# A mixture-of-experts block: the experts' token rows through DRAM tables by indirect DMA in place of one-hot matrices

## The chip, the cores and the metric

One core of one Trainium2 chip runs the whole program; the other cores are idle. The metric is the device time of one execution in microseconds. Three runs of the kernel before took 1461.52, 1463.50 and 1463.19 us; the median is 1463.19.

## The reference

Two transformer layers over 256 tokens of width 1024, in float32: a stick-breaking attention with a dense SwiGLU, then a softmax attention with a mixture of eight experts, then a norm. Only the mixture matters here:

```python
def moe_swiglu(h, w_router, w1, w3, w2):
    t = h.reshape(b * s, d)                       # 256 x 1024
    logits = jnp.dot(t, w_router)                 # 256 x 8
    top_val, top_idx = lax.top_k(logits, TOP_K)   # 2 of 8 experts
    top_w = jax.nn.softmax(top_val, axis=-1)
    gates = jnp.einsum('tk,tke->te', top_w, jax.nn.one_hot(top_idx, N_EXPERTS))

    def expert(args):
        e_w1, e_w3, e_w2, g = args                # 1024x3584, 1024x3584, 3584x1024
        hid = jax.nn.silu(t @ e_w1) * (t @ e_w3)
        return (hid @ e_w2) * g[:, None]
    y = jnp.sum(lax.map(expert, (w1, w3, w2, gates.T)), axis=0)
```

The reference runs all tokens through all experts; a token counts only in its two.

## The kernel before

**Splits.** Each float32 weight tile of 128x1024 is split into a high part (`wh`, ScalarE, line 153) and the remainder (`wl`, VectorE, line 154), and each product is three matmuls of 128x512 (`mm3`, lines 175 to 177): high by high, high by low, low by high. `wh` and `wl` have four buffers each, so the splits run at most four tiles ahead of TensorE.

**Weights.** `jobs` lists the weight loads in the order of use, mostly 1 MB each. `stream()` takes them, and `load_ahead()` issues on SP (line 129) as many as there are buffers `raw`: 9 at first, one more before the second attention (`RING1`), 3 (`RING3`) within it, and 4 (`RING2`) at its end, 17 during the experts. A load waits until VectorE has split the former tile in its buffer. 337 loads belong to the experts, 42 to each whole one.

**Experts.** The core keeps the tokens in two blocks `b` of 128, `hn[b]`, and 128 slots for the tokens of each expert. `slot[:, b, e]` is a token's number within expert `e`, counted from 1, or 0. For expert `e`, `gather()` compares it to `iota` (`mark`, line 808), which gives the one-hot matrix `pe`, and multiplies the blocks by it (line 815), so that the expert's rows come out transposed in PSUM; `split_out` brings them into `eh` and `el`. Each of an expert's seven chunks `i` of 512 hidden columns then does 48 matmuls for `e_w1` and `e_w3`, and 24 for `e_w2` of the chunk before (`down`), into the banks `y`; `hid_t` transposes the hidden tile (line 594). The last chunk of an expert also runs `gather()` of the next. `slots()` transposes `pe` into `pt` (line 845) and works out the gate of each slot (line 847). The first chunk of the next expert ends with `scatter()`: `split_y` multiplies `y` by the gates and splits it (lines 857, 858), eight matmuls by `pt` (lines 870, 871) bring the rows back to their tokens, and four additions (line 872) put them into `ht`. The last expert's rows are scattered after the loop.

**Overflow.** Where an expert has more than 128 tokens, `rest()` runs afterwards under a branch on `most_v` (line 991). With these inputs it doesn't run.

**Order.** The program's text gives the order of dependences; a planner with a simulated timeline places the instructions on each engine's queue, and may move them ahead of ones written earlier. `behind()` fixes an order by hand. GpSimd's queue carries the small loads, the bias tiles and the `rv_d` table.

Of the kernel before, what the change touches and what calls it, by code (L numbers as in the profile page):

```python
# [10 lines left out]
F32 = mybir.dt.float32  # L11
F32R = mybir.dt.float32r
BF16 = mybir.dt.bfloat16
AF = mybir.ActivationFunctionType
ALU = mybir.AluOpType
PSUM = bass.MemoryType.PSUM

P = 128
D = 1024
S = 256  # L20
NB = S // P
# [4 lines left out]
NE = 8  # L26
DFE = 3584
FC = 512
# [2 lines left out]
N_BUCKETS = 32  # L31
MAX_DISTANCE = 128
RING = 9
RING1, RING2, RING3 = 1, 4, 3
GRAN = 2048
HALF = GRAN // 2
NV = 384
WARM = 6
WARMS = 1, 1, 1
MIDDLE = 6  # L40
PUMPS = (7, 7), (7, 7), (7, 7), (7, 7), (2, 3), (2, 3), (1, 3), (2, 2), (2, 2)


@with_exitstack
def block_kernel(ctx: ExitStack, tc: tile.TileContext, x, w_qkv, w_o, mixer_norm, ffn_norm,
                 rel_bias, w1, w3, w2, router, e_w1, e_w3, e_w2, final_norm, onehot, out):
    nc = tc.nc
# [9 lines left out]
    bank = [psp.tile([P, FC], F32, name=f"bank{i}") for i in range(8)]  # L57
# [122 lines left out]
    def split_out(src, h, l):  # L180
        return (nc.scalar.activation(h, src, AF.Copy),  # L181
                nc.vector.tensor_sub(l, src, h.bitcast(F32)))
# [55 lines left out]


    rv_d = dramp.tile([NH, P, NV], F32, name="rv_d")  # L240

    rb = op0.tile([N_BUCKETS, NH], F32, name="rb", bufs=1)
    nc.gpsimd.dma_start(rb, rel_bias)
# [416 lines left out]
    hold = hold[2:]  # L660
    nc.gpsimd.dma_start(rv_d, rv.unsqueeze(1).to_broadcast([NH, P, NV]))
    layer0.close()
    with tc.tile_pool(name="fp", bufs=4) as fp:
        dense_ffn(fp, hold, lambda b: hold.append(norm_t(b, 1)))

# [136 lines left out]
                                           gate[:, b], op0=ALU.mult, op1=ALU.add)  # L802


    def gather(e, banks, later):

        def mark(b):
            return nc.vector.tensor_scalar(pe[:, b], iota, slot[:, b, e:e + 1], None,
                                           op0=ALU.is_equal)

        def part(b, i, later):
            ps = bank[banks[i]]
            for c in range(4):
                cc = 4 * i + c
                i0 = nc.tensor.matmul(ps[:, c * P:(c + 1) * P], hn[b][:, cc * P:(cc + 1) * P],
                                      pe[:, b].bitcast(F32), start=b == 0 and c == 0,
                                      stop=b == NB - 1 and c == 3, skip_group_check=True)
                behind((i0, later))

        def done(i):  # L820
            split_out(bank[banks[i]], eh[:, 4 * i:4 * i + 4].rearrange("p c t -> p (c t)"),
                      el[:, 4 * i:4 * i + 4].rearrange("p c t -> p (c t)"))

        mark(0)
        if e == 0:
            part(0, 0, later)
            later = numbers(1)
            part(0, 1, later)
            held[1] = mark(1)
            for i in range(2):  # L830
                part(1, i, later)
                done(i)
        else:
            mark(1)
            for i in range(2):
                for b in range(NB):
                    part(b, i, later)
                done(i)

    def slots(e):  # L840

# [31 lines left out]
        return i0, i1  # L873

    pend, done = None, None
    gather(0, (3, 4), raws[2])
    k = 0
    most_v = None
    pos2 = mp.tile([P, NB, NE], F32, name="pos2")

    for e in range(NE):
        for i, (f0, n) in enumerate(ecs):
            b1, b3 = (5, 6) if k % 2 == 0 else (3, 4)
            k += 1
            for bk in (b1, b3):
                if bk == b3:
                    held[:] = None, None
                for c, w in enumerate(stream(NC, hold=held)):
                    _, last = mm3(bank[bk], (eh[:, c], el[:, c]), w, c == 0, c == NC - 1)
                if pend is not None and bk == b1:  # L890
                    hT = hid_t(pend[1], FC, bank[pend[2]], *hts)
            if i == len(ecs) - 1 and e + 1 < NE:
                gather(e + 1, (2, 7), last)
            t = gate_mul(ep.tile([P, FC], F32, name="nat"), bank[b1], bank[b3], n)
            if pend is not None:
                for j, w in enumerate(stream(4)):
                    down(y, hT, j, w, pend[0] == 0, pend[0] == len(ecs) - 1)
            pend = (i, t, b1)
            if i == 0:
                if done is not None:  # L900
                    scatter(done)
                else:
                    gates()

                    cps = bank[2]
                    for b in range(NB):
                        nc.tensor.matmul(cps[:, :NE], ones, sel[:, b], start=b == 0,
                                         stop=b == NB - 1)
                    most = mp.tile([P, 1], F32, name="most")
                    nc.vector.tensor_reduce(most, cps[:, :NE], axis=mybir.AxisListType.X,  # L910
                                            op=ALU.max)
                    most_i = mp.tile([P, 1], mybir.dt.int32, name="most_i")
                    nc.vector.tensor_copy(most_i, most)
                    nc.vector.tensor_scalar(pos2, slot, -float(P), None, op0=ALU.add)
                done = slots(e)
    hT = hid_t(pend[1], FC, bank[pend[2]], *(sp[0][:, i * FC:(i + 1) * FC] for i in range(2)))

    row = ep.tile([P, FC], F32, name="nat")
# [143 lines left out]
```

## Time and profile before

| | |
|---|---|
| median of three runs | 1463.19 us |
| profiled execution | 1468.19 us, of which the span from first to last instruction is 1466.5 |
| attention 0, dense layer, attention 1 and routing | 0 to about 460 us |
| eight experts | about 460 to 1447 us |
| last scatter, norm and store | to 1466.5 us |
| TensorE, VectorE, ScalarE busy in 600 to 1340 us | 740.0, 679.4, 578.6 us |
| bytes by DMA | 430 MB, 293 GB/s over the span |

One execution is profiled, so its own time stands beside its span. Busy TensorE is not TensorE at its peak: matmuls overlap, and a 128x512 one is shown with 0.39 us where the next starts 0.23 us later. What an instruction costs TensorE is read from the start of one to the start of the next.

### The profile page before, as it was taken

What the parts mean: (1) busy time and instruction counts of PE and PEld (TensorE: products, weight loads), DVE (VectorE), ACT (ScalarE), POOL (GpSimd) and SP (SyncE); (2) the same over time, 40 slices, a digit from 0 to 9 for tenths busy, and PEclk for the clock granted to TensorE, in tenths of its full rate; (3) what the DMA queues carried; (4) which work ended last, traced back from release to release, by engine and by line L of the source; (5) the groups of instructions that cost most, each with busy time, mean ns of one, the idle gap of its engine ahead of it and who ended that gap; (6) DMA issues with size and microseconds to landing.
All of it is one profiled execution on the core that took longest, in us unless ns stands there. A gap on an engine that the chain in (4) does not pass through costs nothing. (4 is left out here: it accounts for less than half of the span.)

```text
span 1466.5 us, 20171 instructions
## 1 busy us (share of the span) xinstructions
PE 1447.3 (99%) x7553; PEld 1221.5 (83%) x7553; DVE 1203.5 (82%) x1421; ACT 1036.6 (71%) x1303; POOL 21.1 (1%) x44
## 2 busy tenths in 40 slices
PE   9999999999999999999999999999999999999996
PEld 7877999988878888888888888888888888888885
DVE  6555766667667998999999899899999989989995
ACT  6556655546565887787777778777877877877784
POOL 1000000000000000000000000000000000000000
PEclk9999999999998999999999999999999999999998
DMA  9962555556567999999999999999999999999920
GB/s 326 215 235 87 194 186 195 186 178 231 168 229 248 373 366 356 346 368 365 340 345 380 350 348 363 353 344 362 371 348 342 372 355 344 377 360 329 365 92 31
DMA packets 168619, 429.80 MB, mean 293 GB/s; under 512 B 6866, under 2 KB 8946, under 8 KB 154436
## 3 DMA queue, kind: packets, MB, share of 16 engines
q1 hardware_dynamic: 166852, 422.61, 79.9%
q0 software_dynamic: 1600, 5.84, 2.5%
q8 instruction: 61, 1.00, 0.3%
q14 instruction: 42, 0.34, 0.1%
q10 hardware_dynamic: 64, 0.02, 0.0%
HBM read 424.24 MB, written 4.19 MB: 292 GB/s over the span
## 5 line engine op out<-in xcount | busy, mean ns | idle before, releaser
L154 DVE TENSOR_TENSOR wl<-raw,wh 128x1024 fp32r<-128x1024 f32 x710 | 850.6, 1223 | 110.6 <-ACT wh L153 89.3
L153 ACT ACTIVATE wh<-raw 128x1024 fp32r<-128x1024 f32 x710 | 746.3, 1061 | 206.6 <-PE bank L177 165.1
L176 PE MATMUL bank<-wl,oh_t 128*128 128x512 f32 x968 | 377.7, 391 | 0.0
L175 PE MATMUL bank<-wh,oh_t 128*128 128x512 f32 x968 | 374.8, 396 | 0.5 <-ACT oh_t L181 0.5
L177 PE MATMUL bank<-wh,oh_t 128*128 128x512 f32 x904 | 353.6, 391 | 4.0 <-PEq L991 4.0
L176 PEld LDWEIGHTS bank<-wl,oh_t 128*128 128x128 f32 x968 | 182.3, 188 | 38.8 <-DVE wl L154 0.2
L175 PEld LDWEIGHTS bank<-wh,oh_t 128*128 128x128 f32 x968 | 182.9, 189 | 37.9 <-ACT oh_t L181 1.1
L177 PEld LDWEIGHTS bank<-wh,oh_t 128*128 128x128 f32 x904 | 170.4, 189 | 40.3 <-issue 4.2
L177 PE MATMUL bank<-wh,ol_t 128*128 128x512 f32 x504 | 194.4, 391 | 0.0
L162 DVE SCALAR_TENSOR_TENSOR wl<-raw,gcol,wh 128x512 fp32r<-128x512 f32 (+1 forms) x192 | 131.1, 726 | 72.7 <-ACT wh L161 72.3
L161 ACT ACTIVATE wh<-raw,gcol 128x512 fp32r<-128x512 f32 (+1 forms) x192 | 123.9, 699 | 93.6 <-PE bank L313 54.3
L176 PE MATMUL bank<-wl,ol_t 128*128 128x512 f32 x440 | 173.0, 393 | 0.0
L313 PE MATMUL bank<-x_h,wh 128*128 128x256 f32 x512 | 144.7, 283 | 3.4 <-ACT t L435 3.4
L313 PE MATMUL bank<-x_h,wl 128*128 128x256 f32 x512 | 143.8, 281 | 0.0
L313 PE MATMUL bank<-x_l,wh 128*128 128x256 f32 x512 | 143.4, 281 | 0.0
L175 PE MATMUL bank<-wh,ol_t 128*128 128x512 f32 x440 | 140.9, 391 | 0.0
L177 PEld LDWEIGHTS bank<-wh,ol_t 128*128 128x128 f32 x504 | 94.4, 188 | 20.4 <-issue 1.1
L313 PEld LDWEIGHTS bank<-x_h,wh 128*128 128x128 f32 x512 | 96.7, 189 | 5.5 <-ACT t L435 3.6
L313 PEld LDWEIGHTS bank<-x_h,wl 128*128 128x128 f32 x512 | 96.9, 189 | 0.0
L175 PEld LDWEIGHTS bank<-wh,ol_t 128*128 128x128 f32 x440 | 82.6, 188 | 17.1
L313 PEld LDWEIGHTS bank<-x_l,wh 128*128 128x128 f32 x512 | 96.7, 189 | 0.2
L176 PEld LDWEIGHTS bank<-wl,ol_t 128*128 128x128 f32 x440 | 82.9, 188 | 14.9
(199 smaller groups left out, 1201.5 us busy)
## 6 DMA issues: line engine op xcount, KB each, us to landing
raw<-in_e_w_dram SPq DMA_DIRECT2D x335, 1024.0 KB, 6.9
raw<-in_w_dram SPq DMA_DIRECT2D x33, 1024.0 KB, 5.0
raw<-in_w_qkv_dram SPq DMA_DIRECT2D x22, 1024.0 KB, 5.6
raw<-in_w_o_dram SPq DMA_DIRECT2D x8, 1024.0 KB, 9.5
rv_d<-rv POOLq DMA_DIRECT2D x1, 3072.0 KB, 36.2
raw<-in_w_qkv_dram SPq DMA_DIRECT2D x4, 512.0 KB, 7.6
bias<-rv_d POOLq DMA_DIRECT2D x8, 256.0 KB, 4.3
h<-in_x_dram SPq DMA_DIRECT2D x4, 256.0 KB, 6.2
```

Source lines behind the costliest of these rows:

```text
L153: i0 = nc.scalar.activation(wh[:, :m], src, AF.Copy)
L154: i1 = nc.vector.tensor_sub(wl[:, :m], src, wh[:, :m].bitcast(F32))
L161: i0 = nc.scalar.activation(wh[:, cs], src[:, cs], AF.Copy, scale=gc)
L162: i1 = nc.vector.scalar_tensor_tensor(wl[:, cs], src[:, cs], gc, wh[:, cs].bitcast(F32), op0=ALU.mult, op1=ALU.subtract)
L175: i0 = nc.tensor.matmul(ps, s[0], m[0], start=start, stop=False)
L176: nc.tensor.matmul(ps, s[0], m[1], start=False, stop=False)
L177: i1 = nc.tensor.matmul(ps, s[1], m[0], start=False, stop=stop)
L313: nc.tensor.matmul(to, w[a][:, ms], z[:, :, c], start=c + i + m % 2 == 0, stop=c == NC - 1 and m % 2 == 1 and i == 2, skip_group_check=True)
```

## The change

Rows of tokens go through two tables in DRAM. `xs_d` has 128 rows for each of the eight experts, `ys_d` for the first seven. After the first attention `xs_d` is cleared from `hn[1]`, which is free then. Once the slots are known (chunk 0 of expert 0), `send()` works out for each token and each of its two experts the row `128 e + slot - 1` (out of bounds where the slot is above 128) and writes the rows of `hn` there by four indirect DMAs. Expert 1 and later ones load their 128 rows in a plain DMA (`load_x`, in chunk 1 of the expert before), and `turn_x()` transposes them on TensorE, 8 transposes, where `gather()` stood. `store_y()` copies an expert's result to SBUF and stores it in `ys_d`, for experts 0 to 6. In expert 7, `fetch()` clears two tiles and gathers each token's rows by its two row numbers (rows of expert 7 are out of bounds and stay zero), and `add_rows()` adds them, times the gates, to `ht`: block 0 asked for in chunk 2 and added in chunk 3, block 1 in 3 and 4. Expert 0 still gathers, and expert 7 still marks, makes slots and scatters by one-hot matrices. One weight buffer is given up for the two row tiles (`RING2` 4 to 3).

```diff
--- before.py
+++ after.py
@@ -31,13 +31,14 @@
 N_BUCKETS = 32
 MAX_DISTANCE = 128
 RING = 9
-RING1, RING2, RING3 = 1, 4, 3
+RING1, RING2, RING3 = 1, 3, 3
 GRAN = 2048
 HALF = GRAN // 2
 NV = 384
 WARM = 6
 WARMS = 1, 1, 1
 MIDDLE = 6
+FAR = 4096
 PUMPS = (7, 7), (7, 7), (7, 7), (7, 7), (2, 3), (2, 3), (1, 3), (2, 2), (2, 2)
 
 
@@ -238,6 +239,9 @@
 
 
     rv_d = dramp.tile([NH, P, NV], F32, name="rv_d")
+
+    xs_d = dramp.tile([NE * P, D], F32, name="xs_d")
+    ys_d = dramp.tile([(NE - 1) * P, D], F32, name="ys_d")
 
     rb = op0.tile([N_BUCKETS, NH], F32, name="rb", bufs=1)
     nc.gpsimd.dma_start(rb, rel_bias)
@@ -660,6 +664,10 @@
     hold = hold[2:]
     nc.gpsimd.dma_start(rv_d, rv.unsqueeze(1).to_broadcast([NH, P, NV]))
     layer0.close()
+
+    nc.gpsimd.memset(hn[1], 0.0)
+    nc.gpsimd.dma_start(xs_d.rearrange("(e p) d -> p e d", p=P),
+                        hn[1].unsqueeze(1).to_broadcast([P, NE, D]))
     with tc.tile_pool(name="fp", bufs=4) as fp:
         dense_ffn(fp, hold, lambda b: hold.append(norm_t(b, 1)))
 
@@ -802,11 +810,69 @@
                                            gate[:, b], op0=ALU.mult, op1=ALU.add)
 
 
-    def gather(e, banks, later):
-
-        def mark(b):
-            return nc.vector.tensor_scalar(pe[:, b], iota, slot[:, b, e:e + 1], None,
-                                           op0=ALU.is_equal)
+    place = mp.tile([P, NB, NE], F32, name="pos2")
+    row_in = mp.tile([P, 2, NB], mybir.dt.uint32, name="row_in")
+
+    def send():
+
+        nc.gpsimd.iota(rank, pattern=[[0, NB], [P, NE]], base=-1, channel_multiplier=0,
+                       allow_small_or_imprecise_dtypes=True)
+        nc.vector.tensor_scalar(place, slot, float(P), float(FAR), op0=ALU.is_gt, op1=ALU.mult)
+        nc.vector.tensor_add(place, place, slot)
+        nc.vector.tensor_add(place, place, rank)
+        nc.vector.tensor_mul(top, isk, place.unsqueeze(1).to_broadcast([P, 2, NB, NE]))
+        nc.vector.tensor_reduce(tv, top, axis=mybir.AxisListType.X, op=ALU.add)
+        nc.vector.tensor_copy(row_in, tv)
+        for b in range(NB):
+            for k in range(2):
+                nc.gpsimd.indirect_dma_start(
+                    xs_d, bass.IndirectOffsetOnAxis(ap=row_in[:, k, b:b + 1], axis=0), hn[b],
+                    None, bounds_check=NE * P - 1, oob_is_err=False)
+
+    def fetch(b, k):
+
+        t = ep.tile([P, D], F32, name="xr" if k == 0 else "yr")
+        nc.gpsimd.memset(t, 0.0)
+        nc.gpsimd.indirect_dma_start(
+            t, None, ys_d, bass.IndirectOffsetOnAxis(ap=row_in[:, k, b:b + 1], axis=0),
+            bounds_check=(NE - 1) * P - 1, oob_is_err=False)
+        return t
+
+    def add_rows(b, ts):
+        for k, t in enumerate(ts):
+            nc.vector.scalar_tensor_tensor(ht[b], t, ex[:, 1 + k, b:b + 1], ht[b], op0=ALU.mult,
+                                           op1=ALU.add)
+
+    def load_x(e):
+        t = ep.tile([P, D], F32, name="xr")
+        nc.gpsimd.dma_start(t, xs_d[e * P:(e + 1) * P])
+        return t
+
+    def store_y(e):
+        t = ep.tile([P, D], F32, name="yr")
+        nc.scalar.activation(t[:, :FC], y[0], AF.Copy)
+        nc.vector.tensor_copy(t[:, FC:], y[1])
+        nc.gpsimd.dma_start(ys_d[e * P:(e + 1) * P], t)
+
+
+    def mark(e, b):
+        return nc.vector.tensor_scalar(pe[:, b], iota, slot[:, b, e:e + 1], None, op0=ALU.is_equal)
+
+    def take(i, bk):
+        split_out(bank[bk], eh[:, 4 * i:4 * i + 4].rearrange("p c t -> p (c t)"),
+                  el[:, 4 * i:4 * i + 4].rearrange("p c t -> p (c t)"))
+
+    def turn_x(t, banks, later):
+
+        for i in range(2):
+            for c in range(4):
+                cc = 4 * i + c
+                behind((nc.tensor.transpose(bank[banks[i]][:, c * P:(c + 1) * P],
+                                            t[:, cc * P:(cc + 1) * P], ident), later))
+            take(i, banks[i])
+
+    def gather(banks, later):
+
 
         def part(b, i, later):
             ps = bank[banks[i]]
@@ -817,25 +883,14 @@
                                       stop=b == NB - 1 and c == 3, skip_group_check=True)
                 behind((i0, later))
 
-        def done(i):
-            split_out(bank[banks[i]], eh[:, 4 * i:4 * i + 4].rearrange("p c t -> p (c t)"),
-                      el[:, 4 * i:4 * i + 4].rearrange("p c t -> p (c t)"))
-
-        mark(0)
-        if e == 0:
-            part(0, 0, later)
-            later = numbers(1)
-            part(0, 1, later)
-            held[1] = mark(1)
-            for i in range(2):
-                part(1, i, later)
-                done(i)
-        else:
-            mark(1)
-            for i in range(2):
-                for b in range(NB):
-                    part(b, i, later)
-                done(i)
+        mark(0, 0)
+        part(0, 0, later)
+        later = numbers(1)
+        part(0, 1, later)
+        held[1] = mark(0, 1)
+        for i in range(2):
+            part(1, i, later)
+            take(i, banks[i])
 
     def slots(e):
 
@@ -873,10 +928,10 @@
         return i0, i1
 
     pend, done = None, None
-    gather(0, (3, 4), raws[2])
+    gather((3, 4), raws[2])
     k = 0
     most_v = None
-    pos2 = mp.tile([P, NB, NE], F32, name="pos2")
+    pos2 = place
 
     for e in range(NE):
         for i, (f0, n) in enumerate(ecs):
@@ -890,17 +945,18 @@
                 if pend is not None and bk == b1:
                     hT = hid_t(pend[1], FC, bank[pend[2]], *hts)
             if i == len(ecs) - 1 and e + 1 < NE:
-                gather(e + 1, (2, 7), last)
+                turn_x(xr, (2, 7), last)
             t = gate_mul(ep.tile([P, FC], F32, name="nat"), bank[b1], bank[b3], n)
             if pend is not None:
                 for j, w in enumerate(stream(4)):
                     down(y, hT, j, w, pend[0] == 0, pend[0] == len(ecs) - 1)
             pend = (i, t, b1)
             if i == 0:
-                if done is not None:
-                    scatter(done)
+                if e:
+                    store_y(e - 1)
                 else:
                     gates()
+                    send()
 
                     cps = bank[2]
                     for b in range(NB):
@@ -912,7 +968,20 @@
                     most_i = mp.tile([P, 1], mybir.dt.int32, name="most_i")
                     nc.vector.tensor_copy(most_i, most)
                     nc.vector.tensor_scalar(pos2, slot, -float(P), None, op0=ALU.add)
-                done = slots(e)
+            if i == 1 and e + 1 < NE:
+                xr = load_x(e + 1)
+            if e == NE - 1:
+                if i == 0:
+                    for b in range(NB):
+                        mark(e, b)
+                    done = slots(e)
+                elif i == 2:
+                    came = fetch(0, 0), fetch(0, 1)
+                elif i == 3:
+                    add_rows(0, came)
+                    came = fetch(1, 0), fetch(1, 1)
+                elif i == 4:
+                    add_rows(1, came)
     hT = hid_t(pend[1], FC, bank[pend[2]], *(sp[0][:, i * FC:(i + 1) * FC] for i in range(2)))
 
     row = ep.tile([P, FC], F32, name="nat")
```

## Rows read from the trace of the kernel before

**Rows 1.** The page, busy time: us, share of the span, instructions of each engine.
```profile
PE 1447.3 (99%) x7553; PEld 1221.5 (83%) x7553; DVE 1203.5 (82%) x1421; ACT 1036.6 (71%) x1303; POOL 21.1 (1%) x44
```

**Rows 2.** Waits of 600 to 1340 us: us, times, longest; last SP's own.
```profile
ACT wh L153 <- PE bank L177: 113.8, 311, 1.7
...
SPq L129 <- DVE wl L154: 628.3, 251, 5.5
```

**Rows 3.** TensorE's timeline, an expert's last chunk: start us, us, line, operation.
```profile
1064.06 3.73 PE L815 MATMUL bank<-ol_t,hn 128*128 128x128 f32 x32
1067.54 0.48 PE L175 MATMUL bank<-wh,ol_t 128*128 128x512 f32 x1
1067.86 0.40 PE L176 MATMUL bank<-wl,ol_t 128*128 128x512 f32 x1
...
1072.85 0.39 PE L177 MATMUL bank<-wh,ol_t 128*128 128x512 f32 x1
1073.09 0.63 PE L594 MATMUL bank<-ident,nat 128*128 128x128 f32 x4
1073.47 0.47 PE L175 MATMUL bank<-wh,oh_t 128*128 128x512 f32 x1
```

**Rows 4.** TensorE's timeline at the scatters of experts 0 and 6, and slots().
```profile
598.17 0.39 PE L870 MATMUL bank<-ol_t 128*128 128x512 f32 x1
...
1342.70 0.39 PE L870 MATMUL bank<-ol_t 128*128 128x512 f32 x1
...
1343.64 0.63 PE L175 MATMUL bank<-wh,oh_t 128*128 128x512 f32 x2
...
1354.60 0.38 PE L845 MATMUL bank<-ident,ol_t 128*128 128x128 f32 x2
...
1355.18 0.49 PE L176 MATMUL bank<-wl,ol_t 128*128 128x512 f32 x1
```

**Rows 5.** VectorE's groups of 600 to 1340 us: count, busy us, mean ns, idle before.
```profile
L154 DVE TENSOR_TENSOR wl<-raw,wh 128x1024 fp32r<-128x1024 f32 x501 | 599.9, 1223 | 49.9 <-ACT wh L153 34.0
...
L872 DVE TENSOR_TENSOR h<-h,bank 128x512 f32<-128x512 f32 x24 | 15.4, 682 | 0.0
L858 DVE SCALAR_TENSOR_TENSOR ol_t<-bank,gs,yh 128x512 fp32r<-128x512 f32 x12 | 9.0, 748 | 0.2
```

**Rows 6.** Stretches: length, busy us of each engine, granted clock, DMA share, GB/s.
```profile
600.00:1340.00 740.00, 740.00 (x3450) 618.30 (x3449) 679.41 (x645) 578.60 (x621) 0.00 (x0) 1.00 0.98 356
640.00:660.00 20.00, 20.00 (x92) 16.61 (x91) 18.64 (x19) 15.97 (x17) 0.00 (x0) 1.00 1.00 365
10.00:20.00 10.00, 10.00 (x44) 8.06 (x43) 8.42 (x16) 9.92 (x17) 1.12 (x2) 1.00 1.05 388
420.00:430.00 10.00, 10.00 (x50) 7.60 (x49) 5.87 (x22) 6.20 (x16) 0.00 (x0) 1.00 1.05 397
40.00:50.00 10.00, 10.00 (x60) 8.34 (x59) 7.24 (x14) 8.68 (x18) 0.00 (x0) 1.00 1.01 136
150.00:320.00 170.00, 170.00 (x1229) 160.70 (x1228) 108.50 (x146) 87.81 (x125) 0.00 (x0) 1.00 0.58 192
1400.00:1420.00 20.00, 20.00 (x92) 16.61 (x91) 18.47 (x17) 16.06 (x18) 0.00 (x0) 1.00 0.17 57
```

**Rows 7.** GpSimd and VectorE's timeline while expert 0's tokens are routed.
```profile
450.08 2.50 POOL L720 TENSOR_TENSOR hn<-hn,gain 128x512 f32<-128x512 f32 x2
...
451.28 1.84 DVE L717 SCALAR_TENSOR_TENSOR hn<-h,rms,gain 128x512 f32<-128x512 f32 x1
...
458.84 0.16 DVE L792 TENSOR_REDUCE tv<-top 128x2 f32<-128x16 f32 x1
```

**Rows 8.** The page, DMA issues: count, KB each, median us to landing.
```profile
raw<-in_e_w_dram SPq DMA_DIRECT2D x335, 1024.0 KB, 6.9
...
rv_d<-rv POOLq DMA_DIRECT2D x1, 3072.0 KB, 36.2
...
bias<-rv_d POOLq DMA_DIRECT2D x8, 256.0 KB, 4.3
```

## What the change does to the time: the prediction

> **What bounds the kernel now.** I read the busy shares first. TensorE is busy 99% of the span [rows 1], but a busy share alone does not say that it sets the pace, so the second view is the waits of the stage that the change touches, the eight experts (I took 600 to 1340 us, six whole expert periods). There ScalarE's splits wait 113.8 us for matmuls to give back their buffers, and the DMA issues on SP wait 628.3 of 740 us for VectorE to free a buffer [rows 2]. Neither list holds a wait of TensorE, or a wait for a weight load: everybody waits for TensorE, and weights lie ready.
>
> The third view is TensorE's own order of time. From 1067.86 to 1072.85 us there are 22 steps from one 512-column matmul to the next, 0.2268 us each [rows 3]. An expert has 7 chunks of 72 such matmuls, 504, so 114.3 us. The scatters of two experts start at 598.17 and 1342.70 us, six periods apart: 124.09 us each [rows 4]. What stands between 114.3 and 124.1 is also TensorE's: 7 groups of four transposes of the hidden tile at 0.38 us (1073.09 to 1073.47) and about 0.09 us for the slower matmul after each (0.47 for 0.39), 3.3 us; the gather, 3.48 us (1064.06 to 1067.54) and the same 0.09 [rows 3]; the scatter, twice 0.94 us; the transposes and narrow matmuls of slots(), 0.58 us and 0.09 [rows 4]. The sum is 123.7. So under 0.5 us of a period is waiting, and an instruction taken from TensorE in this stage shortens the kernel, as long as the others can follow.
>
> **The change part by part.** Removed from TensorE:
> - gather() for experts 1 to 7, 3.48 us each. turn_x() takes its place with 8 transposes of 128x128. At the 0.095 us of the hidden tile's transposes that is 0.76 us [rows 3]. Saved 2.72 us, seven times: 19.0.
> - scatter() for experts 0 to 6, 8 matmuls, 1.88 us each [rows 4]: 13.2.
> - slots() for experts 0 to 6, 0.67 us each [rows 4]: 4.7. Expert 7 keeps its slots() and scatter(), expert 0 its gather().
>
> Together 36.9 us, all on the path.
>
> VectorE loses four additions of 0.682 us and two splits of 0.748 per expert, 4.2 us [rows 5], and two small marks; store_y() gives it a copy of 128x512, priced as an addition, 0.68. It is busy 679 of 740 us now [rows 6], 113.9 of each period; then about 110.4 of 118.8. The share stays near 93%, so it can follow. ScalarE loses two splits and gets one copy; it has more room (579 of 740).
>
> Expert 7 gets more: add_rows() has four operations of 128x1024 with two inputs from SBUF, priced as the weight split, 1.223 us each [rows 5], two in each of two chunks. A chunk is 16.8 us on TensorE (72 x 0.2268 and 0.47) and 16.0 on VectorE (12 splits, and the product and the split of the hidden tile priced as additions), so 2.45 us more don't fit the chunk. The lower bound is 0: before, 4.2 us of scatter work per expert was taken in without a gap, though with 1.9 us of extra matmuls as cover. The upper bound is what doesn't fit, 2 x 1.6 = 3.3. I take 2.
>
> send() puts six small VectorE operations of some 0.16 us [rows 7] and one iota on GpSimd ahead of or among the first splits of expert 0. There TensorE waits for VectorE before its first matmul. Bounds 0 and 1.2 us (all six on the path, and a hop to GpSimd); I take 0.6, the middle. A GpSimd operation can hold VectorE up: the 128x512 product of 717 takes 1.84 us beside the two GpSimd products that run from 450.08 [rows 7], where L858, of the same size, takes 0.748 [rows 5], so part of this is real. The four 128x1024 memsets of fetch() fall in expert 7 and could do that too; two such products take 2.50 us, and a fill reads nothing, so I leave them inside the 0 to 3.3.
>
> Transfers. GpSimd's queue gets 7 loads and 7 stores of 512 KB, 4 row scatters, 4 row gathers and one 4 MB clearing of the table. It carries nothing in the experts' stage now. No row shows an indirect DMA. Nearest are the bias loads on the same queue, 256 KB in 4.3 us, and the slow end, rv_d, 3 MB in 36.2 us [rows 8], 6 us for 512 KB at its rate. The load of an expert's rows is issued five chunks (84 us) before turn_x() needs them, behind the scatters for expert 1: hidden at either end. The clearing sits in the dense layer, behind the last use of hn[1] there. While rv_d's transfer ran, all transfers together moved only 136 GB/s [rows 6]. At rv_d's rate 4 MB takes 48 us, at the 388 GB/s of a full queue 11. The dense layer draws 192 GB/s [rows 6], so in 48 us 9.2 MB, and its nine buffers hold 9.4. I cost it at nothing; the cover is the full ring, and where it isn't full, a few us are lost.
>
> One weight buffer goes (16 left of 17). A load lands in 6.9 us [rows 8] and a buffer is used up in 2.8, so 16 are 45 us of lead: nothing.
>
> Sum, against the profiled execution: 1468.2 us, of which 1466.5 are span; - 36.9 + 2 + 0.6 = - 34.3, so 1433.9. The profiled execution lies 5.0 us above the median of the runs, so the time to expect is 1463.2 - 34.3 = **1429 us**.
>
> **The rivals.**
> *Transfers become the bound.* An expert moves 44.0 MB of weights (42 loads) and then 1.05 more, in 118.8 us: 380 GB/s, where now it is 356 [rows 6]. For it: the share of the transfer engines is 0.98 already, and in one stretch with share 1.00 they moved 365. Against: when buffers are free all at once they moved 388 and 397 with share 1.05 [rows 6], and now it is the issue that waits for buffers [rows 2]. Since the ring starts full, what counts is the whole stage: 321 loads (337 less 16) and 22 row transfers are 348 MB from 460 us to about 1404 (now the transfers stop soon after 1400 [rows 6], with a full ring ahead of the matmuls): 369 GB/s is enough. At 365 the stage takes 953 us instead of 944, 1438 in all; if the present mean of 356 were a limit, 978, 1463 in all and nothing won.
> The Trainium skill (DMA: Bandwidth & Descriptors, Specifications) speaks against the change here: it gives about 358 GB/s as a core's limit to HBM. By that figure, as an estimate, the stage would take 972 us and the kernel 1457. The stretches at 388 and 397 disagree with it; the mean of 356 would fit it, if the issue did not wait for buffers.
>
> *VectorE takes over the pace.* In the chunk that holds the gather TensorE falls from 20.4 to 17.7 us, while VectorE has 12 splits, two products or splits of 0.68 and the two halves of the expert's rows, 17.4 us [rows 5]. With any handshake between ScalarE and VectorE on top, that chunk is bound by them and the gather's saving is lost: 7 x 2.72 = 19 us, so 1448. Against: the surplus can be taken in by the chunks around it, as the scatter's is now.
>
> *The rows come back late* (slower). VectorE works its queue in order. If an addition of add_rows() is at the head before its rows have landed, all later splits stand behind it, and TensorE behind these. Each of the two rounds has two fills (up to 2.5 us each) and two indirect DMAs of d us, one behind the other, and about a chunk, 16.8 us, to do it in. Lost per round: 2d + 5 - 16.8. With d at 5.9 us or less nothing is lost; the saving of 34.3 is gone from d = 14.5 us on; with d = 20 it loses 56 us, 1485 in all; with rv_d's 36.2 about 120, 1550. For it: no row here has a transfer by a list of rows. Against: 128 rows of 4 KB are a sixth of rv_d's bytes. A smaller lateness, or an order in which the additions stand earlier in the queue, costs up to 10 us or so and leaves the kernel faster.
> The Trainium skill (DMA: Bandwidth & Descriptors, Anatomy of one DMA — SWDGE (gpsimd) path) fits such a transfer at 2.0 us and the bytes at 436 GB/s, an estimate of 3.2 us for 512 KB, by which nothing is lost. The bias loads at 4.3 us for half the bytes are already above that fit.
>
> **How the numbers follow.** About 0.2% (3 us) is what a measurement of this kernel can tell from no change. Forecast 1424 to 1437: 0.70. Transfers bound, 1437 to 1463: 0.08. VectorE's pace, 1437 to 1448: 0.10. Rows a little late, 1437 to 1466: 0.05. Rows late enough to be slower, above 1466: 0.07. Of these about 0.90 is faster, 0.03 the same, 0.07 slower. The range goes from all savings with none of the costs and the rest of the period's 0.4 us, 1423, to the full price of VectorE's pace, 1448.
>
> **What would show it.** On TensorE: 8 transposes in under 1 us where the gather stood, no L870 and L871 but in the last expert, and scatter-free periods of 118.8 us. The waits should still have ScalarE waiting for matmuls, and no wait of ScalarE for a weight load (that would be the first rival). A wait of VectorE for ScalarE in the last chunk of an expert with a gap on TensorE would be the second. A wait of VectorE for the row tiles xr or yr in expert 7, with TensorE idle there, would be the third. I am wrong if the period stays above 121 us, if expert 7 is over 5 us longer than the others' pattern gives, or if the dense layer gets longer, for then the clearing of the table is not covered.

## The result and the profile after

The changed kernel takes 1439.70 us (1439.36 to 1440.46) against 1463.35 us for the kernel before in the same session: a ratio of 0.9837, with an interval of 0.9822 to 0.9852. That is 23.7 us less. The forecast was 34.3 us less, so some 10.6 us of what was taken off TensorE are missing from the time. The profiled execution took 1440.46 us, 1438.7 of them span.

First the page: busy time, and the DMA issues (count, KB each, median us to landing), to be held against [rows 1, 8].

```profile
PE 1420.6 (99%) x7287; PEld 1179.9 (82%) x7287; DVE 1170.3 (81%) x1384; ACT 1009.7 (70%) x1282; POOL 49.7 (3%) x73
...
raw<-in_e_w_dram SPq DMA_DIRECT2D x335, 1024.0 KB, 7.6
...
xs_d<-hn POOLq DMA_DIRECT2D x1, 4096.0 KB, 15.9
xr<-xs_d POOLq DMA_DIRECT2D x7, 512.0 KB, 7.5
ys_d<-yr POOLq DMA_DIRECT2D x7, 512.0 KB, 7.8
```

TensorE is still busy 99%. Two numbers that were open have a row now: the clearing of the table lands in 15.9 us, where the prediction had bounds of 11 and 48, and an expert's rows in 7.5 us.

Next, TensorE's timeline of the changed kernel where turn_x() begins, once per expert (start us, us, line, operation).

```profile
564.22 1.03 PE L870 MATMUL bank<-ident,xr 128*128 128x128 f32 x8
565.01 0.71 PE L176 MATMUL bank<-wh,ol_t 128*128 128x512 f32 x2
...
801.77 1.03 PE L870 MATMUL bank<-ident,xr 128*128 128x128 f32 x8
...
922.74 1.03 PE L870 MATMUL bank<-ident,xr 128*128 128x128 f32 x8
...
1044.36 1.03 PE L870 MATMUL bank<-ident,xr 128*128 128x128 f32 x8
...
1166.00 1.03 PE L870 MATMUL bank<-ident,xr 128*128 128x128 f32 x8
...
1287.50 1.03 PE L870 MATMUL bank<-ident,xr 128*128 128x128 f32 x8
```

The eight transposes take 0.79 us (564.22 to 565.01) where the gather took 3.48 [rows 3]. The first two periods, 564.22 to 801.77, are 118.8 us each: the 124.09 of [rows 4] less the 5.3 us that the prediction took off. The next four are 120.97, 121.62, 121.64 and 121.50 us. So the saving is there in the first experts, and about half of it is lost again from expert 3 on. What waits there? The waits of the changed kernel from 600 to 1340 us (us in total, times, longest), the stretch of [rows 2], without GpSimd's, for which nobody waits in this stretch; SP's own comes last.

```profile
ACT wh L154 <- PE bank L178: 55.7, 175, 0.8
ACT ol_t L182 <- PE bank L177: 54.4, 36, 2.0
...
ACT nat L586 <- PE bank L178: 39.7, 29, 2.3
...
PEld bank L177 <- DVE wl L155: 15.9, 38, 0.8
...
SPq L130 <- DVE wl L155: 627.5, 257, 4.4
```

TensorE's weight loads now wait for a split weight `wl`, which before they never did. And ScalarE's waiting has moved: 113.8 us before weight splits have become 55.7, and 94.1 us lie before the hidden tile's split (182) and Silu (586), up to 2.3 us at a time, where the hidden split alone had 23.9. SP's DMA issues wait for buffers as long as ever, and nobody waits for a weight load.

ScalarE's timeline shows why. First a chunk of expert 2, one of the fast ones, around Silu, then a chunk of expert 4, one of the slow ones (in brackets: idle before, and who ended it).

```profile
710.97 1.06 ACT L154 ACTIVATE wh<-raw 128x1024 fp32r<-128x1024 f32 x1 [0.29 <-PE bank L178]
712.55 1.06 ACT L154 ACTIVATE wh<-raw 128x1024 fp32r<-128x1024 f32 x1 [0.53 <-PE bank L178]
713.52 0.58 ACT L586 ACTIVATE nat<-bank 128x512 f32<-128x512 f32 x1
713.99 2.12 ACT L154 ACTIVATE wh<-raw 128x1024 fp32r<-128x1024 f32 x2
...
947.66 3.90 ACT L154 ACTIVATE wh<-raw 128x1024 fp32r<-128x1024 f32 x4
953.10 0.60 ACT L586 ACTIVATE nat<-bank 128x512 f32<-128x512 f32 x1 [1.53 <-PE bank L178]
953.59 3.89 ACT L154 ACTIVATE wh<-raw 128x1024 fp32r<-128x1024 f32 x4
```

In the fast chunk Silu stands late in the queue: when ScalarE reaches it, its input is there. In the slow one it stands two weight splits earlier. ScalarE stands at it for 1.53 us until TensorE has done the last matmul of the chunk's first matrix, and the splits behind it stand too. Then VectorE's and TensorE's timelines at the same place:

```profile
954.68 3.50 DVE L155 TENSOR_TENSOR wl<-raw,wh 128x1024 fp32r<-128x1024 f32 x3 [1.29 <-ACT wh L154]
...
955.39 0.39 PE L176 MATMUL bank<-wh,oh_t 128*128 128x512 f32 x1
955.96 0.50 PE L177 MATMUL bank<-wl,oh_t 128*128 128x512 f32 x1 [0.18 <-DVE wl L155]
```

VectorE waits 1.29 us for the late `wh`, its `wl` comes late, and TensorE takes a step of 0.57 us where 0.2268 is the rule [rows 3]. The hidden split does the same in the other half of the chunk. The program's text is the same for all these experts; the planner placed the two instructions earlier in the queue from expert 3 on. TensorE's own order turns there as well: the second group of hidden transposes comes 86 matmuls of 512 columns behind turn_x() instead of 92. It does so in e1 and e9 below too, and in e9 without any loss, so that is not what makes the periods long.

The whole span, cut at TensorE's first hidden transposes and at the last matmul for `e_w2` (profiled executions, us):

| | start to first hidden transposes | from there to the last e_w2 matmul | from there to the end | span |
|---|---|---|---|---|
| before | 476.42 | 978.11 | 11.97 | 1466.5 |
| after | 472.93 | 951.12 | 14.65 | 1438.7 |
| after, queue order held (e9 below) | 473.19 | 935.23 | 16.58 | 1425.0 |

The first column changes from one profile to the next (469.5 to 476.4 us over the kernels below), so only the others are read.

### The profile page after: what moved, and what is told of

The parts are those of the page before. It is cut to its first block, busy times and chain, and to the rows that moved or that the text cites. A ratio compares the mean times of both kernels' runs of the same rounds, so it can differ in the third digit from the quotient of the medians.

```text
span 1438.7 us, 19644 instructions
## 1 busy us (share of the span) xinstructions
PE 1420.6 (99%) x7287; PEld 1179.9 (82%) x7287; DVE 1170.3 (81%) x1384; ACT 1009.7 (70%) x1282; POOL 49.7 (3%) x73
## 5 line engine op out<-in xcount | busy, mean ns | idle before, releaser
L155 DVE TENSOR_TENSOR wl<-raw,wh 128x1024 fp32r<-128x1024 f32 x710 | 834.1, 1221 | 113.3 <-ACT wh L154 106.8
L154 ACT ACTIVATE wh<-raw 128x1024 fp32r<-128x1024 f32 x710 | 724.7, 1056 | 131.2 <-PE bank L178 96.7
L177 PE MATMUL bank<-wl,oh_t 128*128 128x512 f32 x968 | 382.4, 396 | 2.3 <-DVE wl L155 2.2
L178 PE MATMUL bank<-wh,ol_t 128*128 128x512 f32 x504 | 194.7, 392 | 0.0
L176 PE MATMUL bank<-wh,ol_t 128*128 128x512 f32 x440 | 137.2, 393 | 0.0
## 6 DMA issues: line engine op xcount, KB each, us to landing
xs_d<-hn POOLq DMA_DIRECT2D x1, 4096.0 KB, 15.9
```

The costliest lines, as they stand in the source:

```text
L154: i0 = nc.scalar.activation(wh[:, :m], src, AF.Copy)
L155: i1 = nc.vector.tensor_sub(wl[:, :m], src, wh[:, :m].bitcast(F32))
L176: i0 = nc.tensor.matmul(ps, s[0], m[0], start=start, stop=False)
L177: nc.tensor.matmul(ps, s[0], m[1], start=False, stop=False)
L178: i1 = nc.tensor.matmul(ps, s[1], m[0], start=False, stop=stop)
```

## The experiments

Theory: the transfers and engines have room for the shorter periods; what makes the late ones long is the place of a few instructions in in-order queues, which the planner chose differently once TensorE's work had changed. Rivals: the loads can't keep up with 118.8 us per expert; VectorE or ScalarE have too much work for it.

**e1_order_held.** The changed kernel with ScalarE's order fixed by hand: the hidden split behind the third weight split of its chunk, Silu behind the last split of the second matrix, and store_y() moved ahead of that hidden split in the text. No work is added or removed.

```diff
+            behind((nc.scalar.activation(t[:, :n], p1[:, :n], AF.Silu), after))
...
+        i0, _ = split_out(ps[:, :n], a[:, :n], c[:, :n])
+        behind((i0, after))
...
+                    third = recent[0] if c == 4 else third if c > 4 else None
+                if bk == b1 and i == 1 and e:
+                    store_y(e - 1, third)
...
+                    hT = hid_t(pend[1], FC, bank[pend[2]], *hts, after=third)
...
+            t = gate_mul(ep.tile([P, FC], F32, name="nat"), bank[b1], bank[b3], n,
+                         after=recent[0])
```

> The changed kernel with the order on ScalarE's queue held by hand: the split of the hidden tile behind the third weight split of a chunk's first matrix, Silu behind the last one of its second matrix, and store_y() moved into the next chunk behind the same third split. In the changed kernel the planner put these two and one splits earlier from expert 3 on, and TensorE's periods went from 118.8 to 121.6 us there. Theory (order of the in-order queue): all periods 118.8 to 119.2, expert 7 some 3 us shorter, 1425 to 1429 us. Rival (transfers or VectorE have no room at this pace): no change, 1437 to 1441. Rival in between (the transposed rows' splits xx still stand early): 1430 to 1435.

Measured: 1428.20 us (1426.84 to 1428.91), ratio 0.9765 (0.9749 to 0.9781). The late periods are 119.4 us instead of 121.6 (from first hidden transposes to first hidden transposes of the next expert); 11.5 us come back from the order alone. A rest of 0.66 us per expert stays from expert 4 on, so not all periods came down to the 118.8 to 119.2 of the theory.

**e2_before_early.** The reverse: the kernel before, with its gather and scatter, but with the hidden split and Silu forced to the early places.

```diff
+                    if c == 3 and bk == b1 and pend is not None:
+                        hT = hid_t(pend[1], FC, bank[pend[2]], *hts, note=held)
+                    if c == 3 and bk == b3:
+                        t = ep.tile([P, FC], F32, name="nat")
+                        held[0] = nc.scalar.activation(t[:, :n], bank[b1][:, :n], AF.Silu)
```

> The kernel before, its arithmetic and tables untouched, with the early order forced: the split of the hidden tile and Silu written after the second weight split of their matrix, and the third held behind them. Theory (order of the queue): ScalarE stands before both in every chunk, TensorE loses 0.2 to 0.5 us per chunk as in the changed kernel's late experts, 56 chunks, so 1474 to 1490 us. Rival (the slow periods come from the change's own faster pace or its transfers, not from the order): 1462 to 1466, as before.

Measured: 1506.48 us (1503.95 to 1508.33), ratio 1.0298 (1.0278 to 1.0318); a chunk is 17.55 us instead of 16.84, in all eight experts. That is 0.7 us per chunk, and the time lies above the 1474 to 1490 that were expected, which went by 0.2 to 0.5 per chunk; why the forced order costs more than the planner's own was not followed up. ScalarE's timeline of this kernel, and the one wait of TensorE's weight loads from 600 to 1340 us:

```profile
1048.06 0.60 ACT L894 ACTIVATE nat<-bank 128x512 f32<-128x512 f32 x1 [1.53 <-PE bank L177]
1048.55 4.91 ACT L153 ACTIVATE wh<-raw 128x1024 fp32r<-128x1024 f32 x5
...
1059.71 0.60 ACT L181 ACTIVATE ol_t<-bank 128x512 fp32r<-128x512 f32 x1 [2.15 <-PE bank L176]
...
PEld bank L176 <- DVE wl L154: 35.1, 75, 0.6
```

The same 1.53 us in front of Silu, in a kernel with no tables, no row loads and slower periods. The early place is enough to make the gaps: 43 us of them.

**e3_before_held.** The kernel before with the holds of e1 on the hidden split and Silu (there is no store_y()).

```diff
+            behind((nc.scalar.activation(t[:, :n], p1[:, :n], AF.Silu), after))
...
+        behind((i0, after))
...
+                    third = recent[0] if c == 4 else third if c > 4 else None
```

> The kernel before with the same holds as e1, which its planner kept by itself: the same order and the same time, 1461 to 1468 us. Its trace also says how the first 100 us of the kernel before vary: the profile of before has TensorE standing 3.6 us at 63 us for a weight load behind the rv_d transfer, the changed kernel's has not. If that is chance, it may be gone here; if it belongs to the kernel before, it stands here too.

Measured, a single run: 1462.35 us, periods of 124.09 us as before. The holds by themselves bring nothing: in the kernel before, the two instructions stood late anyway. The 3.6 us at 63 us are not there, and not in the profile of e8 either, so they belong to the one profiled execution and not to the kernel before.

**e4_one_hot_gather.** e1 with the one-hot gather back for experts 1 to 7; the sends, the clearing, load_x() and turn_x() are gone, the rows' way back stays.

```diff
-                turn_x(xr, (2, 7), last)
+                gather_e(e + 1, (2, 7), last)
...
-            if i == 1 and e + 1 < NE:
-                xr = load_x(e + 1)
```

> e1 with the one-hot gather back for experts 1 to 7 (no xs_d, no clearing, no scatters of rows, no row loads, no turn_x); results still go through ys_d. Theory: the gather's 3.48 us stand again where 0.79 stood, 7 x 2.7 = 18.9 us above e1, 1444 to 1449. If the row table's transfers cost TensorE anything by themselves, the difference to e1 is smaller than 18.9.

Measured: 1442.54 us (1442.42 to 1443.25), ratio 0.9863 (0.9846 to 0.9879), below the 1444 to 1449 of the theory. The periods are 121.47 to 121.49 us, early and late (the last one, which holds expert 7's slots(), 122.19). From 124.09 that is 2.62 for scatter and slots, and down to 118.77 another 2.70 for the gather; the prediction had 2.55 and 2.72. The seven gathers are 18.9 us; from the first hidden transposes to the last this kernel takes 946.21 us and e1 929.92, that is 16.3 us more, the 18.9 less e1's four gaps of 0.66. So the sends, the table and the loads take nothing from that stage. That e1's gaps are missing here does not show that they need the short period: VectorE's copy in store_y(), which makes them (e5 and e9 below), stands one split later in this kernel and never waits.

**e5_rows_held.** e1, and the two splits of the next expert's rows held behind the last split of the down weights in their chunk.

```diff
-            take(i, banks[i])
+            behind((take(i, banks[i]), after))
...
+            ws = [] if pend is None else stream(4)
+            silu = recent[0]
...
+                ws = list(ws)
+                turn_x(xr, (2, 7), last, recent[0])
```

> As the run with the order held, and the splits of the next expert's rows (bank to eh and el) are also held behind the last split of the down weights in their chunk, instead of in the middle of them. Theory (ScalarE's order alone makes the late periods long): the 0.7 us that TensorE still stands per expert from expert 4 on goes, periods of 118.8 us throughout, about 1428.2 - 4 x 0.7 = 1425.4 us. Rival (the rest of the late periods is weights that come late, so the transfers' pace): the gaps move to another place and the time stays at 1428.

Measured: 1427.28 us (1426.61 to 1428.50), ratio 0.9751 (0.9738 to 0.9764), and periods of 119.4 us as in e1: the rival's picture, my guess at the place was wrong. But the gaps didn't wander through the chunk. They all stand at one place, behind another instruction. TensorE's timeline there, and VectorE's:

```profile
943.01 0.39 PE L176 MATMUL bank<-wh,oh_t 128*128 128x512 f32 x1
943.73 0.50 PE L177 MATMUL bank<-wl,oh_t 128*128 128x512 f32 x1 [0.33 <-DVE wl L155]
...
941.85 0.69 DVE L855 COPY yr<-bank 128x512 f32<-128x512 f32 x1 [1.87 <-PE bank L178]
942.45 3.49 DVE L155 TENSOR_TENSOR wl<-raw,wh 128x1024 fp32r<-128x1024 f32 x3
```

VectorE's half of the copy in store_y() stands 1.87 us at the head of its queue for the former expert's last product, with three splits behind it.

**e9_copy_held.** e5, with that copy held behind the last split of its chunk's first matrix.

```diff
-        nc.vector.tensor_copy(t[:, FC:], y[1])
+        behind((nc.scalar.activation(t[:, :FC], y[0], AF.Copy), after),
+               (nc.vector.tensor_copy(t[:, FC:], y[1]), after_v))
```

> As e5_rows_held, and VectorE's half of the copy in store_y is held behind the last split of its chunk's first matrix, as ScalarE's half already is. In e5_rows_held the four gaps left in the late experts (943.01, 1062.44, 1181.86, 1301.99 us on TensorE) each follow that copy, which stands 1.87 us at the head of VectorE's queue until the last product of the expert before is done. Theory (the place in an in-order queue, now VectorE's, makes the gap): no gap there, periods of 118.8 us in experts 3 to 6, 4 x 0.66 = 2.6 us less than 1427.3, so 1424.6 us. Rival (VectorE has too much work in that chunk, so whatever stands last is late): the gap moves to another matmul of the same or the next chunk and the time stays at 1427.

Measured: 1423.98 us (1423.61 to 1426.80), ratio 0.9728 (0.9710 to 0.9746), against 1424.6 expected; the late periods are 118.77 us too (the last one, with expert 7's slots(), 119.49). VectorE's timeline around the same copy, and the row of 600 to 1340 us from the view by stretches (length, busy us of each engine, granted clock, DMA share, GB/s), first of the changed kernel, then of this one:

```profile
939.34 4.63 DVE L155 TENSOR_TENSOR wl<-raw,wh 128x1024 fp32r<-128x1024 f32 x4
...
946.93 0.68 DVE L855 COPY yr<-bank 128x512 f32<-128x512 f32 x1
```

```profile
600.00:1340.00 740.00, 738.71 (x3312) 601.26 (x3311) 662.71 (x618) 570.91 (x621) 10.93 (x15) 1.00 1.01 374
```

```profile
600.00:1340.00 740.00, 740.00 (x3369) 615.62 (x3368) 683.38 (x630) 596.63 (x631) 10.59 (x15) 1.00 1.02 381
```

The copy now comes without a wait, and nothing stands in its place: TensorE is busy all 740 us, its weight loads have no wait left in this stretch. VectorE does more work per time (683 of 740 us) and the loads bring 381 GB/s, so neither work nor transfers bounded the late periods. Against the changed kernel's 0.9837 this is the better version, 15.7 us shorter, with the same work.

**e7_held_14_buffers.** e5 with 14 weight buffers instead of 16.

```diff
-RING1, RING2, RING3 = 1, 3, 3
+RING1, RING2, RING3 = 1, 1, 3
```

> As e5_rows_held with 14 weight buffers in the experts' stage instead of 16. Theory (the loads have room to spare and only the order counts, which is held here): the time of e5_rows_held within 0.2%, periods of 118.8 us. Rival (a stage that lives from the buffers filled ahead, since the transfers are slower than TensorE): the late periods get longer, ScalarE's or VectorE's splits wait for a weight load, and at least 2 MB at 370 GB/s, 5.7 us, are added.

Measured: 1427.48 us (1426.20 to 1427.58), ratio 0.9750 (0.9736 to 0.9765), 0.2 us from e5. The late periods are 119.4 us as in e5, not the 118.8 of the theory: VectorE's copy was not held, and it stands early from expert 3 on, one expert sooner than in e5. With ScalarE's order held, two buffers less cost nothing, so the experts' stage doesn't live from what was loaded ahead.

**e10_plain_14.** The changed kernel, nothing held, with 14 buffers.

```diff
-RING1, RING2, RING3 = 1, 3, 3
+RING1, RING2, RING3 = 1, 1, 3
```

> The changed kernel as it is, nothing held, with 14 weight buffers in the experts' stage instead of 16. Theory (the planner, whose order this is, turns to the early places of the hidden split and of Silu once its own timeline runs out of weights loaded ahead): the order turns at the fourth chunk of expert 2 instead of at the first of expert 3, four more chunks at some 17.3 instead of 16.84 us, about 1439.7 + 1.8 = 1441.5 us; e7_held_14_buffers has the same 14 buffers and lost nothing, so the buffers by themselves are no part of it. Rival (the turn has to do with the rows' loads alone): it turns at the same expert and the time stays at 1439.7.

Measured: 1441.61 us (1440.81 to 1442.68), ratio 0.9850 (0.9828 to 0.9873), against 1441.5 expected. The late periods are 121.7 us, and the first long chunk is the fourth of expert 2 (17.16 us instead of 16.84). By the medians that is 1.9 us more than with 16 buffers, too little to tell apart (the intervals of the ratios overlap), but in the traces the planner turns to the early places sooner. That it turns when its own timeline runs out of weights loaded ahead fits both runs, but the timeline itself is not in the trace; it is argued.

**e6_no_return.** e5 without fetch() and add_rows().

```diff
-                elif i == 2:
-                    came = fetch(0, 0), fetch(0, 1)
-                elif i == 3:
-                    add_rows(0, came)
...
```

> As e5_rows_held, but fetch() and add_rows() of the last expert are left out, so that the contributions of experts 0 to 6 are stored and never added. The difference to e5_rows_held is what the return path costs in the last expert. The prediction's step says 2 us, from 0 to 3.3, by VectorE's 2.45 us too much in each of two chunks. Rival (the cost falls on the chunks around, as for the scatter's work before): under 0.5 us. Second rival (the fills on GpSimd hold VectorE up as well): over 3.3 us.

Measured: 1424.62 us (1423.81 to 1426.32), 2.7 us less than e5, with intervals that overlap (0.9720 to 0.9749 here). It is not the return path alone: the planner also made another order at the end, where five of the last products now stand behind the overflow branch, as twenty do in the kernel before. From the first hidden transposes to the end e6 takes 952.6 us and e5 954.9; of these 2.3 us, 0.7 lie in a chunk of expert 7 and the rest at the end, where the two causes can't be told apart. VectorE's timeline of e5 at the end shows what stands there:

```profile
1407.03 1.28 DVE L844 SCALAR_TENSOR_TENSOR h<-xr,ex,h 128x1024 f32<-128x1024 f32 x1
1408.22 0.74 DVE L914 SCALAR_TENSOR_TENSOR ol_t<-bank,gs,yh 128x512 fp32r<-128x512 f32 x1
1408.88 1.27 DVE L844 SCALAR_TENSOR_TENSOR h<-yr,ex,h 128x1024 f32<-128x1024 f32 x1
```

The additions for block 1 do not stand in the fifth chunk, where the text has them, but between the last splits of `y`. They stand there in the changed kernel and in e9 too.

**e8_before_tail.** The kernel before, with the last 24 matmuls for `e_w2` written ahead of the overflow branch. In the profile of before, TensorE stands at the branch and runs slowly behind it; in the changed kernel those matmuls stand ahead of it. TensorE's timelines, first before, then after:

```profile
1443.01 0.47 PE L176 MATMUL bank<-wl,oh_t 128*128 128x512 f32 x1
1447.44 0.77 PE L177 MATMUL bank<-wh,oh_t 128*128 128x512 f32 x1 [3.95 <-PEq L991]
1448.00 0.63 PE L175 MATMUL bank<-wh,oh_t 128*128 128x512 f32 x1
1448.43 0.63 PE L176 MATMUL bank<-wl,oh_t 128*128 128x512 f32 x1
```

```profile
1424.05 0.39 PE L178 MATMUL bank<-wh,oh_t 128*128 128x512 f32 x1
1426.59 0.50 PE L925 MATMUL bank<-ol_t 128*128 128x512 f32 x1 [2.15 <-DVEq L1060]
```

```diff
+    for half in range(2):
+        for j, w in enumerate(stream(4)):
+            mm3(y[half], hT[j], w, False, j == 3)
...
-        for j, w in enumerate(stream(4)):
-            mm3(y[half], hT[j], w, False, j == 3)
```

> The kernel before with one part alone: the last expert's last 24 matmuls for e_w2 are written ahead of the load of the overflow branch's value instead of behind it, the place that the planner gave them in the changed kernel. Theory: the 2.7 us that the changed kernel gained between the last chunk and the end come from this order, and none of it from the rows' tables: about 1463.5 - 2.7 = 1460.8 us, and the 12 matmuls at half clock behind the branch are gone. Rival (the gain comes from the shorter end of the rows' work): no change, 1463.5 us.

Measured: 1464.55 us (1461.24 to 1468.22), ratio 1.0003 (0.9993 to 1.0013). It settles nothing: the edit changed the text, and the planner put the matmuls behind the branch again, 20 of them as before, so the cause was never varied. Another way of holding them was not tried.

## Why the prediction was right, and where it wasn't

The time lies in the range, 10.7 us above the forecast. In part that is luck: it missed the 1424 to 1437 that had a chance of 0.70, the upper end of the range, 1448, was the price of a rival that is not what happened, and a gain at the end of the kernel that nobody forecast (below) took off some 4 us. The terms on TensorE were right; what failed is the half-sentence at the end of the first part, that an instruction taken from TensorE shortens the kernel "as long as the others can follow".

- *Gather, scatter, slots.* Forecast 2.72, 1.88 and 0.67 us per expert. Measured 2.70 for the gather, 2.62 for scatter and slots of a whole period (e4), and a period of 118.77 us wherever no order is in the way (the first experts, e9). Right.
- *The others can follow.* I asked this of busy shares: VectorE 110.4 of 118.8 us. That was answered rightly, as e9 shows, and it was the wrong question. The splits came late with 7% of VectorE's time to spare, because an instruction stood too early in ScalarE's or VectorE's queue. I took the order of ScalarE's and VectorE's queues as given, while the planner makes it anew for every text and timeline (e6, e8 and e10 show it at other places). The price: between the first hidden transposes and the last e_w2 matmul the changed kernel takes 951.12 us and e9 935.23, 15.9 us lost. From the first turn_x() to the last it is 723.28 against 712.64 us, 10.6 of them in the four late periods; from there to the last product 136.55 against 131.30, the other 5.3, in expert 7.
- *VectorE's pace*, a rival at 1448 us: its mark, TensorE waiting for VectorE, is there, and the time came close to it. But its mechanism, too much work in the chunk that holds the rows, is not what happened: in e9 that chunk is 17.75 us with no wait of TensorE, and the changed kernel's waits lie in other chunks as well.
- *Transfers become the bound.* Fell. The prediction's demand was 380 GB/s and e9 moved 381 over 740 us, with SP's issues waiting for buffers, not for data. The Trainium skill (DMA: Bandwidth & Descriptors, Specifications) gives about 358 GB/s; this trace disagrees, and the measurement decides. The Trainium skill (HBM Reference, Specifications (TRN2)) says that a core that streams alone gets well above that share. In direction the trace agrees with this: the other cores are idle here, and 381 is 6% above.
- *The rows come back late.* Fell. VectorE has no wait for `xr` or `yr` in expert 7. The gathers, the prediction's d, landed 7.9 and 6.3 us after their issue for block 0, beside a full stream of weights, and 4.3 and 6.3 for block 1, and the fills took 0.95 instead of up to 2.5. The 5.9 us at which nothing is lost was not put to the test: the planner placed the additions for block 0 at 1398.7 us, some 70 us after their rows had landed, and those for block 1 at the end of the kernel. The prediction's estimate of 3.2 us by the fit of the Trainium skill (DMA: Bandwidth & Descriptors, Anatomy of one DMA — SWDGE (gpsimd) path) is about half of most of these, and of the 7.5 us of the plain loads.
- *add_rows(), 2 us (0 to 3.3).* Not settled. e6 takes 2.7 us less than e5 by the medians, 2.3 in the profiles, but its end has another order as well. What the traces give to work that doesn't fit a chunk is 0.7 us; the other two additions stand ahead of the last splits of `y`, which the prediction didn't have.
- *send(), 0.6 us, and the clearing, 0.* send() shows no cost, but 0.6 us would hardly be seen: from one same matmul in the second attention to the first hidden transposes it is 81.4 to 82.1 us in three profiles with the kernel before's start and 80.7 to 81.5 in five with send()'s, on average 0.65 less, where expert 0's slots() went, 0.67. The last scatter has landed at about 490 us, 74 us ahead of the first turn_x(). The dense layer, by TensorE's matched instructions, is 187.84 us in the profile of before and in those of e1, e5 and e9, which all clear the table, and 188.22 in the changed kernel's. So the clearing costs nothing, as forecast.
- *The end of the kernel.* Not in the prediction. In the profile of before twenty of the last products stand behind the branch, from 1447.44 us to the end of the experts at 1454.9, and they cost 7.0 us more than their cadence: 4.2 of standing at the branch and 2.7 of thirteen slow steps behind it, most of 0.43 us (granted clock 0.50 in that stretch, the lower level, after TensorE had stood). With these matmuls ahead of the branch that is gone, but TensorE stands there later: from the last product to the scatter's first matmul it is 2.5 us. Between the profiles of before and after the two together gain 4.3 us (7.0, less 14.65 and more 11.97 for the rest); e8 could not show it by itself. This gain hid a part of the loss: 36.9 taken off and 4.3 here, less 15.9, are 25.3 us. The two profiles differ by 24.3 in these stretches, and the medians by 23.7, so about 1 us is not placed; a part of it is a step of 0.68 us that e9 itself still has in expert 7 (at 1395.25 us).

What would have found it: the prediction names "period above 121 us" as its sign of error, and says that the waits would still have ScalarE waiting for matmuls. Both came true. The second was no good as a sign; it should have said before which of ScalarE's instructions.

## What to carry to other kernels

When the engine that bounds is given less work, an automatic order is made anew, and the place of each instruction that waits for that engine counts (in e2 it did without any work taken away). So list, for every in-order queue beside it, the instructions that need the bounding engine's latest result and what stands behind them, and see whether the planner will leave them there. If the new time falls short while busy shares leave room, compare the queues' order between a fast and a slow repetition of the same loop before looking at bandwidth; four fixed places, three of ScalarE's and one of VectorE's, brought back here what the change had promised.

## What the runs showed of the hardware

The four row scatters of the sends follow one another 4.9, 8.4 and 8.9 us apart. GpSimd's timeline of the changed kernel:

```profile
460.67 1.94 POOL L828 DMA_INDIRECT xs_d<-hn,row_in  x1 [7.68 <-DVE gate L809]
465.60 1.03 POOL L828 DMA_INDIRECT xs_d<-hn,row_in  x1 [2.98 <-DMA xs_d<-hn,row_in]
473.96 2.90 POOL L828 DMA_INDIRECT xs_d<-hn,row_in  x1 [7.34 <-DMA xs_d<-hn,row_in]
482.85 0.96 POOL L828 DMA_INDIRECT xs_d<-hn,row_in  x1 [5.99 <-DMA xs_d<-hn,row_in]
```

From the second on each waits for the one before to land, presumably since they write the same table, and each holds GpSimd for 1 to 3 us to issue. Nobody needs GpSimd then, so it costs nothing here. And 4 MB from a broadcast tile of 128 partitions land in 15.9 us, where the broadcast of 3 MB from 16 partitions to `rv_d` takes 36.2 on the same queue [rows 8]; why was not looked into.
